# Streaming-encoder layer on one core: PSUM bank sets of the down products swapped, left halves of the final norm moved into the last product

## The chip, the cores and the metric

The kernel runs on one core of a Trainium2 chip. The metric is the time of one execution in microseconds (us), as the device measures it; lower is better. Three executions of the kernel before took 1205.53, 1206.18 and 1206.33 us.

The engines are named as the profile names them: PE is TensorE (matmuls; PEld are its weight loads), DVE is VectorE, ACT is ScalarE, POOL is GpSimd, SP issues the transfers (DMAs). A line such as L1103 is a line of the kernel before unless the text says otherwise.

## The reference, cut to what matters

The layer is a retention and convolution mixer, then a gated MLP, then a last RMS norm. The change touches only the end of the second part and the norm (SEQ = 1024, D_MODEL = 1024, D_FF = 2816):

```python
def rms_norm(x, g):
    xf = x.astype(jnp.float32)
    y = xf * lax.rsqrt(jnp.mean(xf * xf, axis=-1, keepdims=True) + EPS)
    return (y * g.astype(jnp.float32)).astype(x.dtype)
...
        u = causal_dwconv(h @ w_up, conv_ffn_w, conv_ffn_b)
        ua, ub = jnp.split(u, 2, axis=-1)
        x = x + gt2[:, None, :] * ((jax.nn.silu(ua) * ub) @ w_down)
    return rms_norm(x, final_g)
```

## The kernel before, in words

**Precision.** Every fp32 matmul is three matmuls: each operand is split into a rounded high part (`_h`, a cast on ACT, L99 or L1079) and a low part (`_l`, a subtraction on DVE, L100 or L1080), and `mm3` adds high x high, high x low and low x high.

**Up-projection.** `up` makes one 128-row slice of the MLP at a time: `ua` and `ub` (128 x 1024 each) lie in the two PSUM tiles of `m2k`, two banks each. They are read by the convolution (`conv3`: one activation on ACT, L816, then two multiply-adds on DVE, L85; into `act` from `ua`, into `tb` from `ub`), then by silu and a multiplication (L1001). That is done 22 times; slices are taken in pairs (j, j + 11).

**Down-projection by seven products.** The product of the activations (1024 x 2816) with `w_down` (2816 x 1024) is taken as a 2 x 2 block product with seven block products instead of eight (Strassen's scheme in Winograd's form), numbered 1 to 7. The sums and differences of the quarters are made on DVE in `acts_side` (tiles `sc`) and `weights_side` (tiles `tc`; the weights `wd` are first multiplied by `gt2` on POOL, L1029). All operands are written to DRAM (`keep`, L971). One operand `op_p_j` is a 128 x 1024 tile: left half the activations' side, right half the weights' side.

**A product.** `product(p, ps, start)` runs over j = 0..10. `operands` loads `op_p_j` from DRAM (L1076, a ring of eight buffers; the first three into other tiles), casts it on ACT (L1079) and subtracts on DVE (L1080); there are four buffers for the high parts and four for the low. `step_mm` then does three 128 x 512 matmuls for each of the four row blocks i = 0..3, so 12 per operand and 132 per product. The result of a product is four PSUM banks, one per row block.

**Bank sets.** PSUM has two sets for these: `banks_m` takes the two `m2k` tiles (two row blocks share a tile of two banks), `banks_r` takes four `r1k` tiles of one bank each. The products run in the order 1, 6, 2, 7, 5, 4, 3. Products 1 and 2 accumulate in the set `pa`, 6 in `pb`, 7 and 4 in `pc`, 5 and 3 in `pd`. Before the change `pa` and `pd` come from `banks_m`, `pb` and `pc` from `banks_r`. Waits are set by tile: a matmul into a tile waits for every earlier reader of that tile. Between products ACT copies `pa` to `p1` (L1110), DVE and POOL add results into `x1` (`add_to`, L1103 and L1116).

**The end.** `x1` is the residual stream, eight row blocks `tb` of 128 x 1024. Row blocks 4 to 7 are complete before product 3, row blocks 0 to 3 get their right halves from it. Its last four operands (j = 7..10) are all split first; then for each row block i the 12 matmuls of j = 7..10 are done, so that the blocks finish one after the other. `final(tb)` normalises a row block: square and sum on ACT (L162, a 128 x 1024 activation), two small POOL operations (L156 scale and add, L157 power) that give `r`, one multiplication on DVE by `r` and `fg` (the norm's gain; L1138), and one store (L1139). For row block 3 `final_last` does it in halves (L1141 to L1157): left half squared and multiplied by `fg` early, the right half after its addition, then left half scaled on DVE (L1154), right half on ACT (L1155).

**What sets the order.** The matmuls keep program order; so does everything that is wrapped in `pin`. The rest is ordered by a scheduler when the program is built, each engine's instructions and SP's transfers as one queue in order.

## Time and profile before

| | |
|---|---|
| runs, median (lowest to highest) | 1206.18 us (1205.53 to 1206.33) |
| the profiled execution, its own time | 1208.52 us |
| its span, first to last instruction | 1206.7 us |
| mean granted clock of TensorE | 0.990 |
| busy, share of the span: PE / PEld | 1170.5 us, 97% / 969.9 us, 80% |
| busy: DVE / ACT / POOL | 685.0 us, 57% / 392.0 us, 32% / 208.2 us, 17% |
| bytes moved by DMA | 183.60 MB, mean 152 GB/s |

How to read it: the span and the profiled execution's own time belong to one execution, and differ by what lies around the span; the runs are others. TensorE is busy nearly all the time, but its matmuls overlap and their ends are modelled, so the share does not say that it runs at its pace: the distance between the starts of matmuls does. A granted clock of 1.00 is 2.4 GHz, 0.50 is 1.2 GHz. An idle time is only worth something where TensorE, or the end of the kernel, waits for it.

### The profile page before, as it was taken

To read this page: it belongs to the slowest core of one execution; us is meant where nothing else is said; L and a number is where in the kernel's file an instruction comes from. 1 tells how busy PE (TensorE), PEld (TensorE's weight loads), DVE (VectorE), ACT (ScalarE), POOL (GpSimd) and SP (SyncE) were. 2 spreads that over 40 slices of the span, in tenths; PEclk is the share of its full clock that TensorE was granted. 3 is DMA by queue.
4 is the path that set the end of the run, shared out by engine and by line. 5 is a ranking of instruction groups with operands and counts; after the bars stand their busy time and mean duration, and the time that the engine had idled before them with its cause. 6 is when DMAs were issued, how large, how long until landed. Compare 5 with 4: busy or idle time off the path is not lost. (4 is left out here: it accounts for less than half of the span.)

```text
span 1206.7 us, 13864 instructions
## 1 busy us (share of the span) xinstructions
PE 1170.5 (97%) x5356; PEld 969.9 (80%) x5356; DVE 685.0 (57%) x891; ACT 392.0 (32%) x508; POOL 208.2 (17%) x181
## 2 busy tenths in 40 slices
PE   5999999999999999999999999999999989999996
PEld 5788888888888887788888888888888878888884
DVE  5856577555532677646535555454553664555564
ACT  5760123231221345622222222212222224333352
POOL 3503243100000134410110110110111010430021
PEclk9999999999999999999999999999999989999999
DMA  9932422235411254345525534545453358555552
GB/s 271 291 105 70 140 86 78 84 103 165 144 40 56 92 206 155 106 140 175 184 96 175 192 114 157 183 132 182 157 175 122 140 222 300 192 192 193 193 190 87
DMA packets 135677, 183.60 MB, mean 152 GB/s; under 512 B 6948, under 2 KB 85180, under 8 KB 135612
## 3 DMA queue, kind: packets, MB, share of 16 engines
q1 hardware_dynamic: 135612, 182.72, 45.7%
q8 instruction: 42, 0.69, 0.2%
q14 instruction: 23, 0.19, 0.0%
HBM read 138.13 MB, written 44.56 MB: 151 GB/s over the span
## 5 line engine op out<-in xcount | busy, mean ns | idle before, releaser
L113 PE MATMUL ub<-h,wb_h 128*128 128x512 f32 x704 | 217.7, 390 | 0.0
L113 PE MATMUL ua<-h,wa_h 128*128 128x512 f32 x704 | 217.1, 389 | 0.4 <-DVE h L920 0.3
L113 PEld LDWEIGHTS ua<-h,wa_h 128*128 128x128 f32 x704 | 132.2, 188 | 28.5 <-issue 0.6
L113 PEld LDWEIGHTS ub<-h,wb_h 128*128 128x128 f32 x704 | 132.6, 189 | 27.4
L1080 DVE TENSOR_TENSOR op_l<-ring,op_h 128x1024 fp32r<-128x1024 f32 x74 | 94.3, 1275 | 87.1 <-ACT op_h L1079 87.1
L113 PE MATMUL ub<-h,wb_l 128*128 128x512 f32 x352 | 137.2, 390 | 0.0
L113 PE MATMUL ua<-h,wa_l 128*128 128x512 f32 x352 | 136.9, 389 | 0.0
L1029 POOL TENSOR_TENSOR wd<-wd,gt 128x1024 f32<-128x1024 f32 x22 | 54.4, 2492 | 424.8 <-DMA wd<-in_w_down_dram 424.8
L1079 ACT CAST op_h<-ring 128x1024 fp32r<-128x1024 f32 x74 | 78.1, 1055 | 124.9 <-PE pa L113 38.8
L100 DVE TENSOR_TENSOR wb_l<-wb,wb_h 128x1024 fp32r<-128x1024 f32 x22 | 33.6, 1528 | 136.6 <-ACT wb_h L99 136.6
L113 PE MATMUL po<-wo_h,mix 128*128 128x512 f32 x256 | 82.0, 395 | 0.0
L99 ACT CAST wa_h<-wa 128x1024 fp32r<-128x1024 f32 x22 | 23.2, 1054 | 168.5 <-PE ua L113 168.5
L113 PEld LDWEIGHTS ub<-h,wb_l 128*128 128x128 f32 x352 | 66.2, 188 | 13.8
L113 PEld LDWEIGHTS ua<-h,wa_l 128*128 128x128 f32 x352 | 66.1, 188 | 13.6
L100 DVE TENSOR_TENSOR wa_l<-wa,wa_h 128x1024 fp32r<-128x1024 f32 x22 | 28.4, 1291 | 61.2 <-ACT wa_h L99 61.2
L85 DVE SCALAR_TENSOR_TENSOR tb<-ub,fcol,tb 128x1023 f32<-128x1023 f32 (+1 forms) x44 | 56.2, 1278 | 3.0 <-ACT tb L816 2.3
L85 DVE SCALAR_TENSOR_TENSOR act<-ua,fcol,act 128x1023 f32<-128x1023 f32 (+1 forms) x44 | 56.3, 1279 | 0.8
L113 PEld LDWEIGHTS po<-wo_h,mix 128*128 128x128 f32 x256 | 48.1, 188 | 10.4 <-DVE y L836 0.4
L99 ACT CAST wb_h<-wb 128x1024 fp32r<-128x1024 f32 x22 | 23.2, 1054 | 92.5 <-PE ub L113 92.5
L113 PE MATMUL po<-wo_l,mix 128*128 128x512 f32 x128 | 49.9, 390 | 0.0
L99 ACT CAST wo_h<-wo 128x1024 fp32r<-128x1024 f32 x24 | 25.1, 1049 | 62.5 <-PE pgb L113 16.1
L998 ACT ACTIVATE act<-act 128x1024 f32<-128x1024 f32 x22 | 23.3, 1061 | 61.3 <-DVE act L85 61.3
(266 smaller groups left out, 2370.0 us busy)
## 6 DMA issues: line engine op xcount, KB each, us to landing
ring<-op SPq DMA_DIRECT2D x74, 512.0 KB
wo<-in_w_out_dram SPq DMA_DIRECT2D x24, 512.0 KB
wa<-in_w_up_dram SPq DMA_DIRECT2D x22, 512.0 KB
wb<-in_w_up_dram SPq DMA_DIRECT2D x22, 512.0 KB
op<-sc SPq DMA_DIRECT2D x44, 256.0 KB
wd<-in_w_down_dram SPq DMA_DIRECT2D x22, 512.0 KB
op<-tc SPq DMA_DIRECT2D x44, 256.0 KB
op<-act SPq DMA_DIRECT2D x33, 256.0 KB
```

Of the source, the lines that this page charges most:

```text
L85: return nc.vector.scalar_tensor_tensor(out=o, in0=i0, scalar=s, in1=i1, op0=ALU.mult, op1=ALU.add)
L99: c = nc.scalar.copy(hi, src)
L100: d = nc.vector.tensor_tensor(out=lo, in0=src, in1=hi.bitcast(F32), op=ALU.subtract)
L113: pin(nc.tensor.matmul(ps, st, mv, start=start, stop=stop, skip_group_check=more))
L998: nc.scalar.activation(ta, ta, AF.Silu)
L1029: nc.gpsimd.tensor_tensor(out=t, in0=t, in1=gt2, op=ALU.mult)
L1079: nc.scalar.copy(hi, raw)
L1080: nc.vector.tensor_tensor(out=lo, in0=raw, in1=hi.bitcast(F32), op=ALU.subtract)
```

## The change

It does two things.

1. The bank sets change places: `pa` (products 1 and 2) and `pd` (5 and 3) now come from `banks_r`, one tile per row block; `pb` (6) and `pc` (7 and 4) from `banks_m`.
2. `final_last` is gone, and row blocks 0 to 3 are all normalised in halves. While the last product runs, the left half of each is squared on ACT, its sum scaled on POOL and its values multiplied by `fg` on DVE. After a block's last matmul `out_sum` adds the right half, squares it, makes `r` on POOL and multiplies the right half by `fg`. `out_scale`, called one block later (after the next block's `out_sum`), scales the left half on DVE and the right half on ACT, and stores each half by itself. Nearly all of these are pinned in this order.

```diff
-    pa = banks_m("pa")
+    def square_half(tb, c, junk, name):
+        ss = cst.tile([P, 1], F32, tag="ss", name=name, bufs=6)
+        pin(nc.scalar.activation(junk, x1[:, tb, half[c]], AF.Square, accum_out=ss))
+        return ss
+
+    pa = banks_r("pa")
     product(1, pa, True)
...
-    pb = banks_r("pb")
+    pb = banks_m("pb")
     product(6, pb, True)
...
-    pb = banks_r("pc")
+    pb = banks_m("pc")
     product(7, pb, True)
...
-    pa = banks_m("pd")
+    pa = banks_r("pd")
     product(5, pa, True)
...
-    def final_last(tb, ps):
...
     tail = {j: operands(3, j) for j in range(KB, NK)}
     for tb in range(4, 8):
         final(tb)
+
+    ys, s0 = {}, {}
+    for tb in range(4):
+        ys[tb] = w4(f"y_out_{tb}")
+        s0[tb] = square_half(tb, 0, ys[tb][:, half[0]], f"ss3_{tb}_0")
+        pin(nc.gpsimd.tensor_scalar(out=s0[tb], in0=s0[tb], scalar1=1.0 / D, scalar2=EPS, op0=ALU.mult, op1=ALU.add))
+        l = x1[:, tb, half[0]]
+        pin(nc.vector.tensor_tensor(out=l, in0=l, in1=fg[:, half[0]], op=ALU.mult))
+
+    rs = {}
+
+    def out_sum(tb):
+        pin(add_to(tb, 1, pa[tb]))
+        s1 = square_half(tb, 1, ys[tb][:, half[1]], f"ss3_{tb}_1")
+        r = cst.tile([P, 1], F32, tag="rstd1", name=f"r3_{tb}", bufs=6)
+        pin(nc.gpsimd.tensor_scalar(out=r, in0=s1, scalar1=1.0 / D, scalar2=s0[tb], op0=ALU.mult, op1=ALU.add))
+        pin(nc.gpsimd.tensor_tensor(out=r, in0=r, in1=nhalf[:, 0:1], op=ALU.pow))
+        rs[tb] = r
+        g = x1[:, tb, half[1]]
+        pin(nc.vector.tensor_tensor(out=g, in0=g, in1=fg[:, half[1]], op=ALU.mult))
+
+    def out_scale(tb):
+        y = ys[tb]
+        pin(nc.vector.tensor_scalar(out=y[:, half[0]], in0=x1[:, tb, half[0]], scalar1=rs[tb], scalar2=None, op0=ALU.mult))
+        pin(nc.scalar.activation(y[:, half[1]], x1[:, tb, half[1]], AF.Copy, scale=rs[tb]))
+        for c in half:
+            nc.sync.dma_start(out[tb * P : (tb + 1) * P, c], y[:, c])
+
     for i in range(4):
         for j in range(KB, NK):
             step_mm(pa, tail[j], j, i, False)
-        if i < 3:
-            add_to(i, 1, pa[i])
-            final(i)
-        else:
-            final_last(i, pa[i])
+        out_sum(i)
+        if i:
+            out_scale(i - 1)
+    out_scale(3)
```

The instructions that move stand in three places.

On PE at the start of product 1, the last matmul of the up-projection and the first row blocks of operand 0. Before, with `pa_6909` and `pa_6910` the two tiles of the m set:

```order
L113 MATMUL ub_6819<-h_1_3543,wb_l 128x512
L113 MATMUL pa_6909<-op_0_h 128x512 [waits DVE_49,Activation_49]
L113 MATMUL pa_6909<-op_0_l,op_0_h 128x512
L113 MATMUL pa_6909<-op_0_h,op_0_l 128x512
L113 MATMUL pa_6909<-op_0_h 128x512
L113 MATMUL pa_6909<-op_0_l,op_0_h 128x512
L113 MATMUL pa_6909<-op_0_h,op_0_l 128x512
L113 MATMUL pa_6910<-op_0_h 128x512 [waits DVE_49,Activation_49]
```

Now, with `pa_6909` to `pa_6912` the four tiles of the r set:

```order
L113 MATMUL ub_6819<-h_1_3543,wb_l 128x512
L113 MATMUL pa_6909<-op_0_h 128x512
L113 MATMUL pa_6909<-op_0_l,op_0_h 128x512
L113 MATMUL pa_6909<-op_0_h,op_0_l 128x512
L113 MATMUL pa_6910<-op_0_h 128x512
L113 MATMUL pa_6910<-op_0_l,op_0_h 128x512
L113 MATMUL pa_6910<-op_0_h,op_0_l 128x512
L113 MATMUL pa_6911<-op_0_h 128x512
```

No matmul of operand 0 waits for DVE or ACT any more; the matmuls and their order are the same. In the same way the waits on DVE of the first matmul of row blocks 1 and 3 in product 3's tail are gone.

On DVE at the end of the up-projection, after the two multiply-adds of the last `tb` (L85): `op_3_l` to `op_6_l` are the low parts of product 1's operands, `act` is the last activation, `sc` and `tc` are the sums of its two sides.

```order
 L85 SCALAR_TENSOR_TENSOR tb_6869<-ub_6819,fcol,tb_6869 128x1022
+L1080 TENSOR_TENSOR op_4_l<-ring,op_4_h 128x1024
 L1001 TENSOR_TENSOR act_6868<-act_6868,tb_6869 128x1024
-L1005 TENSOR_TENSOR tc_6896<-wd_10_6890 128x512
+L1005 TENSOR_TENSOR tc_6896<-wd_10_6893,wd_10_6890 128x512
 L1005 TENSOR_TENSOR sc_6878<-act_6868,sc_6878 128x512
 L1005 TENSOR_TENSOR sc_6878<-act_6748,act_6868 128x512
 L1005 TENSOR_TENSOR sc_6878<-act_6868,sc_6878 128x512
-L1005 TENSOR_TENSOR tc_6896<-wd_10_6893,wd_10_6890 128x512
-L1080 TENSOR_TENSOR op_4_l<-ring,op_4_h 128x1024
 L1005 TENSOR_TENSOR tc_6896<-tc_6896,wd_10_6890 128x512
+L1005 TENSOR_TENSOR tc_6896<-wd_10_6890 128x512
+L1005 TENSOR_TENSOR tc_6896<-wd_10_6893,tc_6896 128x512
 L1080 TENSOR_TENSOR op_5_l<-ring,op_5_h 128x1024
-L1005 TENSOR_TENSOR tc_6896<-wd_10_6893,tc_6896 128x512
 L1080 TENSOR_TENSOR op_6_l<-ring,op_6_h 128x1024
```

`op_4_l` moved up by six instructions, the last `tc` moved ahead of `op_5_l`.

On DVE at the very end. Before (L1103 additions, L1138 scaling of a whole row block):

```order
L1103 TENSOR_TENSOR x_2997<-pd_7702,x_2997 128x512 [waits PE_49]
L1138 SCALAR_TENSOR_TENSOR y_out_8291<-x_2997,r_1_8294,fg 128x1024 [waits Activation_49,Pool_49]
L1103 TENSOR_TENSOR x_2997<-pd_7703,x_2997 128x512 [waits PE_49]
L1138 SCALAR_TENSOR_TENSOR y_out_8312<-x_2997,r_2_8315,fg 128x1024 [waits DMAHW7_49,Activation_49,Pool_49]
L1147 TENSOR_TENSOR x_2997<-x_2997,fg 128x512 [waits Activation_49]
L1103 TENSOR_TENSOR x_2997<-pd_7703,x_2997 128x512 [waits PE_49]
L1150 TENSOR_TENSOR x_2997<-x_2997,fg 128x512 [waits Activation_49]
L1154 TENSOR_SCALAR y_out_last<-x_2997,r_last 128x512 [waits DMAHW0_49,Pool_49]
```

Now (lines of the changed kernel; L1173 is the product with `fg`, L1177 the scaling of a left half):

```order
L1103 TENSOR_TENSOR x_2997<-pd_7702,x_2997 128x512 [waits PE_49]
L1173 TENSOR_TENSOR x_2997<-x_2997,fg 128x512 [waits Activation_49]
L1177 TENSOR_SCALAR y_out_8262<-x_2997,r_1_8311 128x512 [waits Pool_49]
L1103 TENSOR_TENSOR x_2997<-pd_7703,x_2997 128x512 [waits PE_49]
L1173 TENSOR_TENSOR x_2997<-x_2997,fg 128x512 [waits Activation_49]
L1177 TENSOR_SCALAR y_out_8267<-x_2997,r_2_8334 128x512 [waits DMAHW7_49,Pool_49]
L1177 TENSOR_SCALAR y_out_8272<-x_2997,r_3_8357 128x512 [waits DMAHW0_49,Pool_49]
```

The scaling of a block now stands behind the next block's addition, not ahead of it, and is half as wide.

## Rows read from the trace of the kernel before

**Rows 1.** Waits of PE: engine, line, waited for: us in total, times, longest us

```profile
PE pa L113 <- DVE tb L85: 3.4, 1, 3.4
PE pd L113 <- DVE x L1103: 3.2, 2, 2.4
```

**Rows 2.** Timeline of PE, product 1: start us, us, line, operation [idle before <-releaser]

```profile
978.14 0.39 PE L113 MATMUL pa<-op_h 128*128 128x512 f32 x1
...
979.27 0.39 PE L113 MATMUL pa<-op_h,op_l 128*128 128x512 f32 x1
983.08 0.76 PE L113 MATMUL pa<-op_h 128*128 128x512 f32 x1 [3.42 <-DVE tb L85]
...
1014.65 0.39 PE L113 MATMUL pb<-op_h 128*128 128x512 f32 x1
```

**Rows 3.** Windows at product 1: stretch, us, busy of PE, PEld, DVE, ACT, POOL, PEclk, DMA

```profile
980.00:983.00 3.00, 0.00 (x0) 0.00 (x0) 2.93 (x4) 0.27 (x1) 0.95 (x1) 0.90 1.02 415
983.00:984.00 1.00, 0.92 (x2) 0.83 (x3) 1.00 (x1) 0.00 (x0) 1.00 (x1) 0.50 0.45 176
...
990.00:995.00 5.00, 5.00 (x24) 4.11 (x23) 5.00 (x7) 2.11 (x2) 0.00 (x0) 1.00 1.04 383
```

**Rows 4.** Timeline of DVE after the last up-projection

```profile
980.34 2.59 DVE L85 SCALAR_TENSOR_TENSOR tb<-ub,fcol,tb 128x1023 f32<-128x1023 f32 x2
982.97 2.53 DVE L1001 TENSOR_TENSOR act<-act,tb 128x1024 f32<-128x1024 f32 x1
985.42 2.88 DVE L1005 TENSOR_TENSOR tc<-wd 128x512 f32<-128x512 f32 x1
...
991.77 0.68 DVE L1005 TENSOR_TENSOR tc<-tc,wd 128x512 f32<-128x512 f32 x1
992.37 1.21 DVE L1080 TENSOR_TENSOR op_l<-ring,op_h 128x1024 fp32r<-128x1024 f32 x1
```

**Rows 5.** Timeline of POOL in the same stretch

```profile
982.05 5.70 POOL L1029 TENSOR_TENSOR wd<-wd,gt 128x1024 f32<-128x1024 f32 x2 [46.14 <-DMA wd<-in_w_down_dram]
```

**Rows 6.** Timeline of PE, product 3: its first matmul, and its tail

```profile
1164.26 0.39 PE L113 MATMUL pd<-op_h 128*128 128x512 f32 x1
...
1183.30 0.39 PE L113 MATMUL pd<-op_h 128*128 128x512 f32 x1
...
1187.38 0.50 PE L113 MATMUL pd<-op_h 128*128 128x512 f32 x1 [0.78 <-DVE x L1103]
...
1192.72 0.39 PE L113 MATMUL pd<-op_h,op_l 128*128 128x512 f32 x1
1195.53 0.50 PE L113 MATMUL pd<-op_h 128*128 128x512 f32 x1 [2.42 <-DVE x L1103]
...
1198.19 0.39 PE L113 MATMUL pd<-op_h,op_l 128*128 128x512 f32 x1
```

**Rows 7.** Timeline of DVE in product 3 and at the end

```profile
1174.54 1.28 DVE L1138 SCALAR_TENSOR_TENSOR y_out<-x,r,fg 128x1024 f32<-128x1024 f32 x1 [0.44 <-POOL r L157]
...
1197.65 1.29 DVE L1138 SCALAR_TENSOR_TENSOR y_out<-x,r,fg 128x1024 f32<-128x1024 f32 x1 [2.18 <-POOL r L157]
...
1199.46 0.68 DVE L1103 TENSOR_TENSOR x<-pd,x 128x512 f32<-128x512 f32 x1
...
1202.42 0.49 DVE L1154 TENSOR_SCALAR y_out_last<-x,r_last 128x512 f32<-128x512 f32 x1 [0.80 <-POOL r_last L1153]
```

**Rows 8.** Windows in product 3 and at the end, columns as in rows 3

```profile
1150.00:1180.00 30.00, 30.00 (x134) 24.85 (x133) 20.56 (x20) 15.79 (x19) 8.15 (x8) 1.00 0.51 181
...
1193.00:1195.50 2.50, 0.11 (x1) 0.00 (x0) 1.89 (x2) 0.00 (x0) 0.55 (x1) 1.00 0.00 0
...
1199.00:1203.00 4.00, 0.00 (x0) 0.00 (x0) 2.32 (x4) 1.30 (x3) 1.24 (x2) 0.73 0.33 131
```

**Rows 9.** Timelines of SP and ACT: loads of product 1's operands from `op_8` on, and its cast

```profile
994.58 25.65 SPq L1076 DMA_DIRECT2D ring<-op  x16
...
998.73 1.05 ACT L1079 CAST op_h<-ring 128x1024 fp32r<-128x1024 f32 x1 [1.86 <-DMA ring<-op]
```

More of the change, by code (lines that the diff above doesn't have):

```diff
@@ L1139, in final @@
         nc.sync.dma_start(out[tb * P : (tb + 1) * P, :], y)
-    def final_last(tb, ps):
-        y = w4("y_out_last")
-        xs = x1[:, tb]
-        ss = [cst.tile([P, 1], F32, name=f"ss3_last_{i}") for i in range(2)]
-        nc.scalar.activation(y[:, half[0]], xs[:, half[0]], AF.Square, accum_out=ss[0])
-        nc.gpsimd.tensor_scalar(out=ss[0], in0=ss[0], scalar1=1.0 / D, scalar2=EPS, op0=ALU.mult, op1=ALU.add)
-        nc.vector.tensor_tensor(out=xs[:, half[0]], in0=xs[:, half[0]], in1=fg[:, half[0]], op=ALU.mult)
-        add_to(tb, 1, ps)
-        nc.scalar.activation(y[:, half[1]], xs[:, half[1]], AF.Square, accum_out=ss[1])
-        nc.vector.tensor_tensor(out=xs[:, half[1]], in0=xs[:, half[1]], in1=fg[:, half[1]], op=ALU.mult)
-        r = cst.tile([P, 1], F32, name="r3_last")
-        nc.gpsimd.tensor_scalar(out=r, in0=ss[1], scalar1=1.0 / D, scalar2=ss[0], op0=ALU.mult, op1=ALU.add)
-        nc.gpsimd.tensor_tensor(out=r, in0=r, in1=nhalf[:, 0:1], op=ALU.pow)
-        nc.vector.tensor_scalar(out=y[:, half[0]], in0=xs[:, half[0]], scalar1=r, scalar2=None, op0=ALU.mult)
-        nc.scalar.activation(y[:, half[1]], xs[:, half[1]], AF.Copy, scale=r)
-        for c in half:
-            nc.sync.dma_start(out[tb * P : (tb + 1) * P, c], y[:, c])
     KB = NK - 4
```

## The prediction

> **What bounds the kernel now.** I read the waits of TensorE first, since it is busy for 97% of the span: what it waits for is nearly all that can be won. Two waits of that list lie where the change works: 3.4 us in product 1 on VectorE's `tb` (the convolution that reads the last `ub`), and 3.2 us in two pieces, the longer 2.4, on the additions of line 1103 [rows 1].
>
> Then the timeline of TensorE at product 1. The reader is to see that the six matmuls of blocks 0 and 1 go, the last at 979.27, that the third block starts only at 983.08, and that the next product starts at 1014.65 [rows 2]. At full pace 84 matmuls of product 3 take 1164.26 to 1183.30, 0.2267 us each, so an operand (12) takes 2.72 and a product (132) 29.92 [rows 6]. Product 1 took 1014.65 - 978.14 = 36.51, so it lost 6.59. Only 3.81 - 0.23 = 3.58 of that is the gap; the windows show the rest: the granted clock is 0.90 over 980 to 983, 0.50 (1.2 GHz) in 983 to 984, and 1.00 (2.4 GHz) again from 990 [rows 3]. So about 3.0 us are the half clock after the pause.
>
> Last the tail, where product 3 finishes block after block. Block 1 starts at 1187.38 after a wait, and from 1192.72 to 1195.53, block 2 to block 3, it is 2.81 instead of 0.23 [rows 6]. From 1183.30 to 1198.19 stand 47 steps, 10.65 at full pace and 14.89 in fact: 4.24 lost, of which about 0.4 is the late `op_10` in block 0. After the last matmul (1198.19 + 0.39) the addition that needs it starts only at 1199.46, since VectorE scales block 2 from 1197.65 on [rows 7].
>
> **The change, part by part.** *The swap at product 1.* `pa` now lies in the r banks, free since before the up-projection, and the two waits at its start are gone. The 6.59 go, unless operands are late next. An operand is needed every 2.72 us from 978.14 and its low part one matmul later. The first three were split early, `op_3` before 980.34 [rows 4]. `op_4`, now ahead of the last multiplication of the activations, is needed at 989.2 and takes the place of the row 982.97 to 985.42 [rows 4]: in time. `op_5` is what I expect late. Between the end of `tb` at 982.97 and `op_5` VectorE does the same work as before in another order, plus one subtraction of `tc` that stood behind `op_5`: 992.37 - 991.77 = 0.60 more. Before, `op_5` started at 992.37 [rows 4]; now at 992.97, done with 1.21 at 994.2. TensorE wants it at 978.14 + 5 x 2.72 + 0.23 = 991.97 and resumes at about 994.3: a stall of 2.3. Bounds: none, if VectorE is less held up than before (it lost some 3.5 us there: 2.53 and 2.88 where such work takes 1.2 and 0.68 [rows 4], beside GpSimd's two multiplications [rows 5]), and 3.6, if it is held until these end at 987.75 and has 1.2 + 1.2 + 7 x 0.60 + 1.21 = 7.8 left, to 995.5. I take 2.3, because the rows show this very work.
> The Trainium skill bears on that wait ("SBUF — State Buffer", Who interferes with whom): a VectorE instruction with two SBUF inputs and a GpSimd one that reads SBUF exclude each other for a whole instruction. The rows agree in size, 2.88 - 0.68 = 2.2 beside 5.70 for two. By that rule at its hardest the stall is 3.6, and the sum below 1.3 us worse.
>
> After it `op_6` and the rest need 1.2 each in 2.72: VectorE catches up. The swap at the other products costs nothing: each set was read a whole product earlier. Reading m-bank blocks in pairs delays an addition by one block, 0.7 us, with a product's 29.92 to spare.
>
> *The tail.* One tile per bank takes away both waits on line 1103: 4.24 - 0.4 = 3.8 us. The last addition no longer queues behind a 1.29 us scaling: 1199.46 - 1198.58 = 0.88, less 0.05 for the signal, 0.8 more. In the new order VectorE's work for a block (addition, product with `fg`, the half scaling of the block before) is some 1.7 us in a block's 2.72, so it is idle when block 3 ends. The chain behind the last addition (square, two operations on GpSimd, scaling, transfer) is the old one.
> Against it: the half scaling of block 2 (0.49, as the row at 1202.42 [rows 7]) now stands before the last scaling and may hold GpSimd's power, 0 to 0.49, I take 0.2; and block 2's output leaves about 1 us before block 3's, not 4: 0 to 1 us, I take 0.2, as the two halves start apart. Sum of the tail: 3.8 + 0.8 - 0.4 = 4.2.
>
> *The four early half squares and products.* ScalarE gets four squares of 512 columns, each under the 1.05 of a 1024-column cast [rows 9], VectorE four products of 0.60, both between 1170 and 1182. In 1150 to 1180 they are busy 15.79 and 20.56 of 30 us [rows 8], so the idle time is cover: 14.2 and 9.4. The tightest is `op_8`: before, the scaling with `r_7` ended at 1174.54 + 1.28 = 1175.8 [rows 7]; I allow 1.5 more for its later square, then `op_6`, a product, `op_7`, three products and `op_8` (3 x 1.2 + 4 x 0.60 = 6.0) end at 1183.3, and it is wanted at 1183.30 + 3 x 0.2267 + 0.23 = 1184.2. If that cover is gone, block 0 stalls by that much, at most 2.4. GpSimd's four added `ss` operations stand behind the last `r_7`, and nothing waits for them before block 0's square. The two later `y_out` buffers wait for the stores of `y_out_4` and `y_out_5`; ScalarE stops there with `op_7` behind it, needed some 8 us later. The queue of transfers has eight half stores for four others at the end: eight issues of about 0.4 us in some 11 us.
>
> **The sum.** 6.6 - 2.3 + 4.2 = 8.5 us. The profiled execution took 1208.52 (span 1206.7, 1.8 around it), so such a one would show 1200.0. The runs' median lies 2.3 below it, at 1206.18; the same difference gives **1197.7**. About 0.2%, 2.4 us, is what a measurement of this kernel tells from no change.
>
> **The rivals.** *The clock falls in the new stall.* For it: after the 3.58 pause it was at half for some 6 us, costing 3.0. Against it: the 2.58 pause of the tail (2.81 - 0.23) left it at 1.00 [rows 8]. But the idle stretch after the last matmul has 0.73 over 1199 to 1203 [rows 8], so it fell there between 2 and 3 us after the work ended. A stall of 2.3 lies at the edge. Price 1.5 to 3.0, taken as 3.0: 1200.7. The skill ("TensorE: Matmul & The Clock Gate", HAM oscillation) says that waits between bursts of matmuls put the array back to the low clock and each burst starts cold; by that rule 1200.7 is the time. The pause of product 1 agrees, the pause of the tail doesn't.
>
> *No stall.* If VectorE isn't held up, `op_5` comes in time: 8.5 + 2.3 = 10.8, 1195.4. The rows of that work speak against it.
>
> *Only one of the gains.* VectorE is held to the bound of 3.6 and the clock falls by 3.0: the pause only moves and the tail's 4.2 are left, 1202.0. (That is the lock of the skill's SBUF page with its clock rule.) Or the tail waits on something new and the start's 4.3 are left: 1201.9.
>
> *Slower.* One transfer decides it: product 1 reads `op_9` from DRAM, and that load is issued behind the last store of `tc`, about 993.6. Its low part is ready at 993.6 + L + 1.05 + 1.23 and wanted at 978.14 + 9 x 2.72 + 2.3 + 0.23 = 1005.2: late if its landing L is over 9.3. The nearest row, `op_8` issued at 994.58 and cast at 998.73 [rows 9], gives L = 4.15. With L = 18 the stall is 8.7, and 3.0 for the clock: 11.7 - 8.5 = 3.2 slower, 1209.4. From L of 17 it is over the bound. Only a transfer four times as slow would do it.
>
> That the change doesn't do what it says is excluded for the waits: the instruction order has none where they were.
>
> **How the numbers follow.** Forecast 0.45; clock falls 0.30; no stall 0.08; one gain alone 0.13; slower 0.04. The first three lie within 1195.4 and 1200.7; with the bounds of the tail (0.4 below, 1.3 above) the range is 1195.0 to 1202.0, which leaves out the slower case and some of the one before it. Faster by over 0.2% is all but the last case and a rest for several bounds together: 0.93; within 0.2% 0.03; slower 0.04.
>
> **What would show it.** Right: the waits of TensorE have no `pa` on `tb` and no `pd` on line 1103; the third block of product 1 starts at 978.6; a wait of about 2.3 on `op_l` before `op_5`, then steady 2.72 steps; product 1 takes about 32.2; the tail's 47 steps take about 11, and the last addition starts within 0.1 of the last matmul. The clock around 994 to 1000 tells forecast from first rival. Wrong: `op_l` waits at other operands, in the tail above all, a wait on `ring`, or ScalarE waiting for a store at `y_out`.

## The result and the profile after

| | before | after |
|---|---|---|
| runs beside each other, median (lowest to highest) | 1206.11 us (1205.53 to 1206.33, 4 runs) | 1196.99 us (1196.71 to 1199.93, 4 runs) |
| ratio | | 0.9934, 95% interval 0.9922 to 0.9947 |
| the profiled execution: own time, span | 1208.52, 1206.7 us | 1197.04, 1195.2 us |

The change makes the kernel faster by 0.5 to 0.8%, well over the 0.2% that can be told; the forecast was 1197.7 us, with a range of 1195.0 to 1202.0. Of every kernel one execution was profiled, so a row below tells of that execution.

The head of the page after. TensorE's work is what it was, 5356 matmuls, in 11.5 us less; VectorE has 6 instructions more than its 891 before, ScalarE 9 more than its 508.

```profile
span 1195.2 us, 13885 instructions
...
PE 1166.3 (98%) x5356; PEld 967.5 (81%) x5356; DVE 687.8 (58%) x897; ACT 394.1 (33%) x517; POOL 212.8 (18%) x184
```

The only wait of TensorE in the changed kernel, from the start of product 1 to the end, as the waits list it (columns as in [rows 1]). Both waits of [rows 1] are gone; this one is new.

```profile
PE pa L113 <- DVE op_l L1080: 1.9, 1, 1.9
```

TensorE in product 1 after (columns as in [rows 2]). The third block starts 1.36 us after the first, at full pace, where it had waited 3.42. The new wait stands before the second matmul of `op_5`, which wants its low part: 990.65 - 988.32 = 2.33 where a step is 0.23. Product 1 takes 1006.88 - 974.72 = 32.16 instead of 36.51.

```profile
974.72 0.39 PE L113 MATMUL pa<-op_h 128*128 128x512 f32 x1
...
976.08 0.39 PE L113 MATMUL pa<-op_h 128*128 128x512 f32 x1
...
988.32 0.39 PE L113 MATMUL pa<-op_h 128*128 128x512 f32 x1
990.65 0.50 PE L113 MATMUL pa<-op_l,op_h 128*128 128x512 f32 x1 [1.95 <-DVE op_l L1080]
...
1006.88 0.39 PE L113 MATMUL pb<-op_h 128*128 128x512 f32 x1
```

The windows around this wait (columns as in [rows 3]): the granted clock stays at 1.00 (2.4 GHz) through the wait and behind it, where [rows 3] had 0.50.

```profile
985.00:990.00 5.00, 3.70 (x17) 2.73 (x15) 5.00 (x9) 2.10 (x2) 0.00 (x0) 1.00 0.80 297
990.00:992.00 2.00, 1.35 (x6) 1.13 (x7) 2.00 (x3) 0.00 (x0) 0.00 (x0) 1.00 1.03 382
992.00:994.00 2.00, 2.00 (x11) 1.65 (x10) 2.00 (x2) 0.00 (x0) 0.00 (x0) 1.00 1.06 340
994.00:996.00 2.00, 2.00 (x11) 1.65 (x10) 0.00 (x1) 0.00 (x0) 0.00 (x0) 1.00 1.08 264
```

VectorE in front of the wait, then GpSimd beside it. The reader is to see that VectorE has no idle time from the last `tb` to the end of `op_5` (the first of the four `op_l` in the last row), and that two instructions there are long: the subtraction of `op_4` with 2.47 and the last multiplication of the activations with 3.42. The same two kinds take 1.23 (at 964.89) and 1.22 (at 957.78) elsewhere. Beside them GpSimd works on the last pair's weights.

```profile
976.92 2.60 DVE L85 SCALAR_TENSOR_TENSOR tb<-ub,fcol,tb 128x1023 f32<-128x1023 f32 x2
979.43 2.47 DVE L1080 TENSOR_TENSOR op_l<-ring,op_h 128x1024 fp32r<-128x1024 f32 x1
981.82 3.42 DVE L1001 TENSOR_TENSOR act<-act,tb 128x1024 f32<-128x1024 f32 x1
985.17 0.68 DVE L1005 TENSOR_TENSOR tc<-wd,wd 128x512 f32<-128x512 f32 x1
...
988.78 0.68 DVE L1005 TENSOR_TENSOR tc<-wd,tc 128x512 f32<-128x512 f32 x1
989.38 4.62 DVE L1080 TENSOR_TENSOR op_l<-ring,op_h 128x1024 fp32r<-128x1024 f32 x4
```

```profile
978.41 5.75 POOL L1029 TENSOR_TENSOR wd<-wd,gt 128x1024 f32<-128x1024 f32 x2 [45.89 <-DMA wd<-in_w_down_dram]
```

TensorE in product 3 after, against [rows 6]: first matmul; then blocks 0, 1, 2 and 3 of the tail; last matmul. The tail's 47 steps take 11.09 where they took 14.89; 0.41 of the 0.44 that is still lost lies in block 0, whose 12 steps take 1178.65 - 1175.52 = 3.13 instead of 2.72, since `op_10` is late there.

```profile
1156.47 0.39 PE L113 MATMUL pd<-op_h 128*128 128x512 f32 x1
...
1175.52 0.39 PE L113 MATMUL pd<-op_h 128*128 128x512 f32 x1
...
1178.65 0.40 PE L113 MATMUL pd<-op_h 128*128 128x512 f32 x1
...
1181.39 0.39 PE L113 MATMUL pd<-op_h 128*128 128x512 f32 x1
...
1184.12 0.39 PE L113 MATMUL pd<-op_h 128*128 128x512 f32 x1
...
1186.61 0.39 PE L113 MATMUL pd<-op_h,op_l 128*128 128x512 f32 x1
```

VectorE behind the last matmul (L1173 is the product with `fg`, L1177 the scaling of a left half, first of block 2 and then of block 3). The addition starts 0.42 after the start of the last matmul, 0.03 after its end at 1187.00; the last scaling starts 3.02 after the addition, as in [rows 7] (2.96), and the span ends 5.15 after that, where it was 4.28.

```profile
1187.03 0.69 DVE L1103 TENSOR_TENSOR x<-pd,x 128x512 f32<-128x512 f32 x1
1188.51 0.69 DVE L1173 TENSOR_TENSOR x<-x,fg 128x512 f32<-128x512 f32 x1 [0.79 <-ACT y_out L1107]
1189.12 0.49 DVE L1177 TENSOR_SCALAR y_out<-x,r 128x512 f32<-128x512 f32 x1
1190.05 0.49 DVE L1177 TENSOR_SCALAR y_out<-x,r 128x512 f32<-128x512 f32 x1 [0.43 <-POOL r L1170]
```

So the end of the kernel falls into six stretches that can be compared over all kernels of this study, each from the same kind of row: the start of product 1; product 1 (to the first matmul of product 6); the products between (to the first matmul of product 3); product 3 (first to last start of a matmul); from there to the start of the last addition; to the start of the last scaling; to the end of the span.

| kernel | product 1 starts | product 1 | between | product 3 | to the addition | to the scaling | to the end | product 1 to the end |
|---|---|---|---|---|---|---|---|---|
| before | 978.14 | 36.51 | 149.61 | 33.93 | 1.27 | 2.96 | 4.28 | 228.56 |
| after | 974.72 | 32.16 | 149.59 | 30.14 | 0.42 | 3.02 | 5.15 | 220.48 |
| e1, swap alone | 974.21 | 34.26 | 149.60 | 30.13 | 1.00 | 5.46 | 4.04 | 224.49 |
| e2, tail alone | 976.04 | 35.23 | 149.60 | 32.28 | 0.43 | 3.01 | 4.41 | 224.96 |
| e3, `op_5` early | 977.14 | 32.20 | 149.60 | 30.13 | 0.42 | 3.02 | 5.19 | 220.56 |
| e4, left halves stored early | 977.34 | 32.51 | 149.60 | 30.13 | 0.43 | 2.97 | 5.22 | 220.86 |
| e5, weights early | 975.01 | 29.92 | 149.60 | 30.13 | 0.42 | 3.02 | 4.60 | 217.69 |
| e6, whole stores | 975.92 | 32.40 | 149.60 | 30.12 | 0.43 | 3.01 | 5.32 | 220.88 |
| e7, e5 and a longer ScalarE | 975.84 | 29.91 | 149.61 | 30.12 | 0.43 | 3.01 | 4.58 | 217.66 |
| e8, e5 and a longer VectorE | 972.84 | 29.92 | 149.60 | 30.14 | 0.42 | 3.02 | 4.26 | 217.36 |
| e9, after and a longer VectorE | 975.09 | 32.34 | 149.60 | 30.13 | 0.43 | 3.02 | 4.29 | 219.81 |
| e10, the kernel of e8 again | 973.22 | 29.92 | 149.60 | 30.16 | 0.43 | 3.02 | 4.25 | 217.38 |

The views give the span to a tenth, so the last two columns are good to 0.05.

The part that was changed gained 228.56 - 220.48 = 8.08 us. The two profiled executions differ by 11.5; the other 3.4 lie ahead of product 1, where the programs do the same work. That start moves from execution to execution: it lies between 974.21 and 978.14 in seven kernels (before, after, e1 to e4, e6) whose up-projection was left alone. Most of it comes early: after 1000 matmuls TensorE is at 212.6 us before and at 209.4 after, so 3.2 of the 3.4 are lost by then, and over all twelve kernels that point lies between 208.1 and 212.6. A part comes near 500 us, where the granted clock drops to 0.50 (1.2 GHz) in nine kernels and stays at 1.00 (2.4 GHz) in e1, e5 and e8: from that point to product 1 these three take 763.8 to 764.3, the others 765.1 to 765.8. A median of four to seven executions carries some of all that, so the experiments are read from the stretches, and from the medians only where these differ by more.

### The profile page after: what moved, and what is told of

The parts are those of the page before. It is cut to its first block, busy times and chain, and to the rows that moved or that the text cites. A ratio compares the mean times of both kernels' runs of the same rounds, so it can differ in the third digit from the quotient of the medians.

```text
span 1195.2 us, 13885 instructions
## 1 busy us (share of the span) xinstructions
PE 1166.3 (98%) x5356; PEld 967.5 (81%) x5356; DVE 687.8 (58%) x897; ACT 394.1 (33%) x517; POOL 212.8 (18%) x184
## 4 chain that ended last, share of the span: by engine, by line
PE 89%; DVE 4%; issue 2%; POOL 2%; ACT 2%; DMA 1%; SPq 1%; POOLq 0%; DVEq 0%
PE ub L113 20%; PE ua L113 20%; PE po L113 5%; PE pc L113 5%; PE pd L113 5%; PE pa L113 4%; PE pg L113 4%; PE pq L113 4%; PE pk L113 4%; PE pgc L113 4%; PE phc L113 4%; PE pgb L113 4%; PE pb L113 3%; PE pv L113 2%; POOL x L904 1%
## 5 line engine op out<-in xcount | busy, mean ns | idle before, releaser
L85 DVE SCALAR_TENSOR_TENSOR tb<-ub,fcol,tb 128x1023 f32<-128x1023 f32 (+1 forms) x44 | 56.2, 1278 | 3.0 <-ACT tb L816 2.3
L85 DVE SCALAR_TENSOR_TENSOR act<-ua,fcol,act 128x1023 f32<-128x1023 f32 (+1 forms) x44 | 56.3, 1280 | 0.8
```

Source lines behind the costliest of these rows:

```text
L85: return nc.vector.scalar_tensor_tensor(out=o, in0=i0, scalar=s, in1=i1, op0=ALU.mult, op1=ALU.add)
```

## The experiments

**e1: the swap alone.** The kernel before, with its old tail and the bank sets exchanged.

```diff
-    pa = banks_m("pa")
+    pa = banks_r("pa")
...
-    pb = banks_r("pb")
+    pb = banks_m("pb")
...
-    pb = banks_r("pc")
+    pb = banks_m("pc")
...
-    pa = banks_m("pd")
+    pa = banks_r("pd")
```

> The bank sets swapped, the old tail (whole row blocks scaled at once, halves for block 3 alone). Theory: the swap alone takes away both places where TensorE waited, the start of product 1 (4.3 us won) and the two waits on line 1103 in the tail (3.8), since one tile per bank is all that these need. TensorE's list of waits then has no pa on tb and no pd on x, and the last matmul comes as early as with the whole change; what is lost is behind the last matmul: the scaling of block 2 (1.28 us, after its own square and power) stands ahead of block 3's last steps, some 2.4 us later than with the new tail. Expected about 1199, 7 us faster than before. Rival: the waits in the tail need the late scaling of the new tail code too; then the two waits (3.2 us) stay and the time is 1201 to 1202.

Measured: 1200.66 us (1200.49 to 1201.63, 5 runs), ratio 0.9958 (0.9946 to 0.9970). Product 3 takes 30.13, with no wait on L1103: the swap by itself takes both waits out of the tail, and the rival, that they need the new code too, falls. Without the new code the last scaling comes 6.46 after the start of the last matmul, where the changed kernel has 0.42 + 3.02 = 3.44, so 3.02 later (2.4 were expected): VectorE and ScalarE work through block 2's norm and both halves of block 3 first. The last two additions are one row of e1, and the last one, the second of the two, starts at 1189.20:

```profile
1188.60 1.28 DVE L1103 TENSOR_TENSOR x<-pd,x 128x512 f32<-128x512 f32 x2
```

And product 1 takes 34.26, 2.10 more than after, with a wait that is 0.48 longer; that is why the time lies above the 1199 that were expected. TensorE's row and the windows of e1 show it:

```profile
990.63 0.50 PE L113 MATMUL pa<-op_l,op_h 128*128 128x512 f32 x1 [2.43 <-DVE op_l L1080]
```

```profile
990.00:991.00 1.00, 0.37 (x2) 0.33 (x3) 1.00 (x2) 0.00 (x0) 0.00 (x0) 1.00 1.04 381
991.00:992.00 1.00, 1.00 (x6) 0.82 (x5) 1.00 (x2) 0.00 (x0) 0.00 (x0) 0.98 1.02 381
992.00:994.00 2.00, 2.00 (x7) 1.52 (x6) 1.98 (x2) 0.00 (x0) 0.00 (x0) 0.50 1.08 332
994.00:996.00 2.00, 2.00 (x7) 1.59 (x6) 0.00 (x0) 0.00 (x0) 0.00 (x0) 0.66 0.90 266
```

After a wait of 2.43 the granted clock fell to 0.50 (1.2 GHz), some 1.3 us after the matmuls had resumed. That is the prediction's first rival, met in this kernel.

**e2: the tail alone.** The changed kernel with the four bank sets put back.

```diff
-    pa = banks_r("pa")
+    pa = banks_m("pa")
...
-    pa = banks_r("pd")
+    pa = banks_m("pd")
```

> The new tail on the old bank sets. Theory: product 1 loses its 6.6 us as before (pause on tb, then half clock), and in the tail TensorE still waits twice on line 1103, because two row blocks share a tile, but only for an addition that starts at once, some 0.8 us of idle time each instead of 0.8 and 2.4: TensorE's tail is 1.6 to 1.9 us shorter than before, and the last addition no longer queues (0.8). Less about 0.9 for the two stores that collide at the end: 1.5 to 2.5 us faster than before, about 1204. Rival: the tail code is what makes the tail short, whatever the banks: then 3.7 us faster than before, 1202.4, and no wait over 0.5 us on line 1103.

Measured: 1202.77 us (1200.74 to 1204.01, 7 runs), ratio 0.9971 (0.9960 to 0.9982). The waits of TensorE in e2:

```profile
PE pa L113 <- DVE tb L85: 3.4, 1, 3.4
...
PE pd L113 <- DVE x L1103: 1.6, 2, 0.8
```

The pause of product 1 is back as it was, 3.42 long. The clock behind it is not: the granted clock is at 0.50 from 982.4 to 989.2 before and only from 981.2 to 984.6 in e2. A window of e2 and one of the kernel before, some 5 and 4 us after the matmuls have resumed (at 980.98 and 983.08):

```profile
986.00:990.00 4.00, 4.00 (x20) 3.28 (x19) 4.00 (x6) 1.35 (x2) 0.34 (x1) 1.00 0.50 187
```

```profile
987.00:990.00 3.00, 3.00 (x10) 2.32 (x9) 3.00 (x4) 0.06 (x1) 0.75 (x1) 0.63 0.33 122
```

So product 1 takes 35.23 instead of 36.51, and e2 is 3.6 us faster than before, by its time where the rival put it (3.7). Its waits are those of the theory: from product 3's start to the end it gains 2.31, within the 1.5 to 2.5 expected, and the other 1.28 is the clock. In the tail the two waits are now 0.8 each instead of 0.8 and 2.4: with the scaling behind the next addition the longer one shrinks, and only the swap takes away the rest. Both parts of the change work on the same waits of L1103, so their gains there don't add: e1 gains 3.80 in product 3, e2 1.65, both together 3.79.

**e3: `op_5` ahead of the last sums.** The last pair's sums are emitted behind product 1's first six operands.

```diff
...
-        acts_side(j, acts[j], acts[j + NK])
-        weights_side(j)
+        if j < NK - 1:
+            acts_side(j, acts[j], acts[j + NK])
+            weights_side(j)
...
-    product(1, pa, True)
+    product(1, pa, True, range(6))
+    acts_side(NK - 1, acts[NK - 1], acts[2 * NK - 1])
+    weights_side(NK - 1)
+    product(1, pa, True, range(6, NK))
```

> The changed kernel with the first six operands of product 1 written ahead of the last pair's sums, so that on VectorE the low part of operand 5 stands directly behind the last multiplication of the activations and ahead of the sums sc and tc. Theory: the 1.95 us wait of product 1 (2.1 with what follows it) is the order of VectorE alone; it goes, and nothing takes its place, as the low part of operand 6 ends about when it is wanted (991.2 against 991.3 in the changed kernel's time). Expected 1194.7 to 1195.2, product 1 in 29.9 to 30.3 us. Rival: the work in front of operand 6 is the same as it was in front of operand 5, so the wait only moves to operand 6 or 7 and the time stays at 1197; second rival: the later sums delay the stores and the loads of operands 9 and 10, and TensorE waits there on ring.

Measured: 1195.91 us (1195.05 to 1199.44, 5 runs), ratio 0.9917 (0.9903 to 0.9931). The wait before `op_5` is gone, but product 1 takes 32.20 as before it: two shorter waits of 0.70 and 0.77 stand before `op_6` and `op_9`. The median is 1.1 below that of the changed kernel and its lowest run too, yet from product 1 to the end it takes 220.56 against 220.48, so this is no gain. The theory, 29.9 to 30.3 for product 1, falls; the rival, that the wait moves on, is what happened. VectorE in e3 tells where the time goes:

```profile
981.85 3.41 DVE L1081 TENSOR_TENSOR op_l<-ring,op_h 128x1024 fp32r<-128x1024 f32 x1
985.18 3.42 DVE L1001 TENSOR_TENSOR act<-act,tb 128x1024 f32<-128x1024 f32 x1
988.53 1.21 DVE L1081 TENSOR_TENSOR op_l<-ring,op_h 128x1024 fp32r<-128x1024 f32 x1
```

It is not the place of `op_5` in the order: the subtraction of `op_4` and the last multiplication are long again. Moving work behind them only moves the wait.

**e5: the last pair's weights early.** What makes them long? GpSimd's two multiplications, or something else in that stretch (the transfers, the casts)? e5 calls the weights' side of the last pair before its up-projection.

```diff
     for j in range(NK):
+        if j == NK - 1:
+            weights_side(j)
         for i in range(2):
...
-        weights_side(j)
+        if j < NK - 1:
+            weights_side(j)
```

> The changed kernel with one thing moved: the weights' side of the last pair (its two loads, GpSimd's two multiplications, the four sums tc and their stores) is emitted before the last two up-projection slices instead of behind them. Theory (VectorE is slow at op_4 and at the last multiplication of the activations because GpSimd's two multiplications run beside them, and the tc sums lie between them and op_5): the two VectorE instructions that took 2.47 and 3.42 us go back to about 1.2 each, op_5's low part is ready well before TensorE wants it, the wait of 1.95 us before op_5 is gone, product 1 takes 29.9 to 30.3 us instead of 32.16, and from the start of product 1 to the end it is 218.2 to 218.6 us instead of 220.48; the time is about 1195. Rival 1 (those two instructions are slow for another reason, the transfers or ScalarE's cast beside them): they still take over 2 us each; then only the four sums leave the path and the wait shrinks without the durations doing so. Rival 2 (the lock only moves): an instruction of the convolution beside GpSimd's multiplications takes 2 to 4 us instead of 1.2 and TensorE waits for it in the up-projection, so that what product 1 gains is lost before it.

Measured: 1193.48 us (1192.78 to 1194.46, 4 runs), ratio 0.9895 (0.9877 to 0.9913). VectorE behind the last `tb`, then GpSimd, whose two multiplications for this pair (the last of the three, and the one alone) now end 23 us ahead of product 1 instead of 9 behind its start:

```profile
979.72 1.22 DVE L1083 TENSOR_TENSOR op_l<-ring,op_h 128x1024 fp32r<-128x1024 f32 x1
980.86 1.22 DVE L1001 TENSOR_TENSOR act<-act,tb 128x1024 f32<-128x1024 f32 x1
981.99 1.22 DVE L1083 TENSOR_TENSOR op_l<-ring,op_h 128x1024 fp32r<-128x1024 f32 x1
```

```profile
928.41 8.10 POOL L1029 TENSOR_TENSOR wd<-wd,gt 128x1024 f32<-128x1024 f32 x3 [38.75 <-DMA wd<-in_w_down_dram]
949.55 2.39 POOL L1029 TENSOR_TENSOR wd<-wd,gt 128x1024 f32<-128x1024 f32 x1 [13.04 <-DMA wd<-in_w_down_dram]
```

The two instructions take 1.22 each, `op_5` is split from 981.99 on, done at 983.2 where TensorE wants it at 988.8, and product 1 takes 29.92, its full pace. Rival 1 falls, since the two are short with a cast of ScalarE still beside them (at 980.65) and the DMA engines busier than in the changed kernel (0.58 of the stretch 979.72 to 983.20, against 0.49 of 979.43 to 985.24). So does rival 2: the list of TensorE's waits is empty from 880 to the end. The first of the two multiplications does meet a busy VectorE (933.12 to 936.51 in the trace, 3.39 instead of 2.39), but no instruction of the convolution beside it takes more than 1.28. From product 1 to the end e5 takes 217.69, 0.5 below what was expected: the last stretch is shorter too, 4.60 instead of 5.15, which was not forecast.

**e4: left halves stored early.** The other term to look into is the 0.87 at the end. First guess: block 2's store collides with block 3's. e4 scales and stores each block's left half by itself, right behind the next block's addition, and the right half later.

```diff
...
-            out_scale(i - 1)
-    out_scale(3)
+            out_right(i - 1)
+    out_left(3)
+    out_right(3)
```

> The changed kernel with the scaling of a left half placed directly behind the next block's addition on VectorE (ahead of its product with fg), its store issued there. Block 2's left half is then stored about 1.4 us earlier. Theory: the end of the changed kernel, 5.15 us from the last scaling to the end against 4.28 before, is longer because block 2's two stores still move when block 3's are issued; with one of them out of the way the stretch falls to 4.3 to 4.8 and the time by 0.4 to 0.9, to 1196.1 to 1196.6. Rival: two half stores at the end take as long as that by themselves (their last one is issued late or lands slowly): the stretch stays at 5.1 and the time at 1197. TensorE's part of the tail is untouched by it.

Measured: 1200.25 us (1196.67 to 1201.24, 6 runs), ratio 0.9946 (0.9932 to 0.9961); from product 1 to the end 220.86. The last stretch takes 5.22, though block 2's left half now leaves ahead of the rest. That speaks against the collision as the cause. The median lies 3.3 above that of the changed kernel, which neither guess had; in the profiled execution (1199.95) 2.62 of it are the later start of product 1.

**e6: whole stores.** The profile's DMA part for the last 6 us has something else. After, with the share of the DMA engines and the rate in 40 slices of 0.15 us:

```profile
DMA  0000089998999969999999991000000000000000
GB/s 0 0 0 0 0 328 410 382 423 328 396 396 396 314 219 355 355 369 410 355 355 423 369 342 28 14 14 27 14 27 0 0 0 0 0 0 0 0 0 0
...
q1 hardware_dynamic: 576, 1.05, 47.5%
q14 instruction: 1, 0.01, 0.3%
```

The stores run at full rate up to the 24th slice, then bytes trickle in at 14 to 28 GB/s for six slices, 0.9 us. And there is one packet of what the profile calls an instruction queue (q14), 2.9 us before the end, which the last 6 us of the kernel before do not have. Which engine's program is it? e6 stores blocks 0 to 2 whole, which takes three transfers out of SP's program.

```diff
-        for c in half:
+        for c in half if tb == 3 else (slice(0, 1024),):
             nc.sync.dma_start(out[tb * P : (tb + 1) * P, c], y[:, c])
```

> The changed kernel with row blocks 0 to 2 stored whole (one transfer of 512 KB each, three instructions fewer on SP); block 3 still in halves. In the changed kernel the last scaling starts 5.15 us before the end, in the kernel before 4.28, and its profile has a packet of the instruction queue 2.85 us before the end, which the kernel before has not; behind it the bytes of the stores trickle in at 14 to 27 GB/s for 0.8 us. Theory (the packet, a piece of some engine's program, holds one DMA engine up, and it is there because a program has grown): if SP's program is the one that grew over an edge, the packet is gone and the last scaling starts 4.3 us before the end, 0.8 less, about 1196.1; if ScalarE's or another's is, the packet and the 5.15 stay, within 0.2. Rival (block 2's store collides with block 3's): now block 2's store starts later, when both its halves are scaled, so that more of it lies beside block 3's; the last scaling starts 5.2 to 5.6 us before the end and no trickle of one engine is seen.

Measured: 1198.51 us (1194.55 to 1199.39, 6 runs), ratio 0.9931 (0.9914 to 0.9948). The packet stays, 2.7 us before the end, the trickle too, and the stretch takes 5.32. SP has as many instructions as in the kernel before (783 in the trace), so it is not SP's program. The 5.32 lies where the rival, the collision, had it too (5.2 to 5.6); the trickle speaks against that, and e9 decides.

**e7 and e8: which program.** In e5 the stretch was 4.60 and no packet lay in it, with the same tail. e7 and e8 are e5 with eight small copies that nothing uses, on ScalarE or on VectorE.

```diff
+    dummy = cst.tile([P, 8], F32, name="dummy")
...
+            for n in range(8):
+                nc.scalar.copy(dummy[:, n : n + 1], nhalf[:, 0:1])
```

(In e8 the last line is `nc.vector.tensor_copy` with the same operands. In both the scheduler put the copies near the start.)

> e5 (last pair's weights early) with eight copies of one element per partition added to ScalarE's program, which nothing uses. In e5 the packet of the instruction queue at the end is gone and the last scaling starts 4.60 us before the end, though it has the same tail and as many instructions that compute; only waits that are instructions of their own are fewer: the trace has 802 instructions of ScalarE against 807 in the changed kernel, 1217 of VectorE against 1218, and 794 and 1217 in the kernel before. Theory (ScalarE's program is the one that grew over the edge, between 802 and 807): with 810 the packet is back in the last 6 us, a trickle of one engine follows the stores, and the last scaling starts 5.1 to 5.3 us before the end; product 1 stays at 29.9. Rival (it is VectorE's program, between 1217 and 1218, or chance): no packet at the end, 4.5 to 4.7 us.

> e5 with the same eight copies added to VectorE's program instead. Theory (ScalarE's program): no packet of the instruction queue in the last 6 us, the last scaling starts 4.5 to 4.7 us before the end. Rival (VectorE's program is the one that grew over the edge): the packet is back and the last scaling starts 5.1 to 5.3 us before the end. If neither this run nor the one with ScalarE's copies shows the packet, it does not hang on the length of a program and its cause stays open.

Measured: e7 1195.30 us, e8 1192.01 us (one run each). The theory of ScalarE falls: with 810 instructions no packet came back, and the stretch stayed at 4.58. VectorE's copies did move a packet, but not as the rival had it: it now lies at 1171.4, 19 us before the end, and the stretch takes 4.26. With all kernels set side by side, the last packet follows the count of VectorE's instructions (all in the trace, with those that only wait or signal, which the head of a page leaves out):

| VectorE's instructions in the trace | kernels | last packet of the instruction queue, against the end of the span |
|---|---|---|
| 1214 | e1 | 1.3 us behind it |
| 1217 | before, e5, e7 | 0.6, 0.6 and 0.3 us behind it |
| 1218 | after, e3, e4, e6 | 2.9, 3.0, 2.8 and 2.7 us ahead of it |
| 1221 | e2 | 4.8 us ahead |
| 1225 | e8, e10 | 18.8 and 18.9 us ahead |
| 1226 | e9 | 18.9 us ahead |

**e9: the changed kernel with a longer VectorE program.** The same eight copies, in the changed kernel itself.

```diff
+    dummy = cst.tile([P, 8], F32, name="dummy")
+    for n in range(8):
+        nc.vector.tensor_copy(dummy[:, n : n + 1], nhalf[:, 0:1])
```

> The changed kernel itself with eight copies of one element per partition, used by nothing, added to VectorE's program near its start. So far the last packet of the instruction queue stood, in seven kernels, where VectorE's count of instructions says: with 1214 1.2 us behind the end, with 1217 0.1 to 0.6 behind it, with 1218 2.7 to 3.1 us before it, with 1221 4.9 before it, with 1225 19 us before it; ScalarE's count does not order them. Theory (the packet is a piece of VectorE's program, asked for when VectorE comes to a certain instruction, and costs time only where it meets the last stores): with 1226 it lies about 20 us before the end, and the last scaling starts 4.2 to 4.6 us before the end instead of 5.15; product 1 stays near 32.2 to 32.5 with its wait for op_5; from the start of product 1 to the end about 219.7 to 220.2 us. Rival (the 0.87 comes of the half stores colliding, and e5 lost it only by its other timing): the packet moves but the last scaling still starts 5.1 to 5.3 us before the end.

Measured: 1197.06 us (1193.82 to 1198.98, 4 runs), ratio 0.9922 (0.9901 to 0.9942). The last 6 us of e9:

```profile
GB/s 410 301 14 0 0 0 0 0 0 0 96 382 355 369 423 383 382 369 382 301 232 369 396 382 396 355 396 382 396 232 14 0 0 0 0 0 0 0 0 0
...
q1 hardware_dynamic: 645, 1.16, 51.8%
```

No packet, no trickle: the stores run at full rate to their end, and the last scaling starts 4.29 before the end of the span, as in the kernel before, with the same eight half stores in the same order. Eight instructions more make the stretch 0.86 shorter, and the rival, that the half stores collide, falls. The packets of the trace say where the 0.86 lies: the last bytes of the stores end 2.9 us after the start of the last scaling in before, e1, e5 and e7 to e10, 3.0 in e2, 3.6 to 3.7 in after, e3 and e4, and 4.1 in e6. The q14 packet itself is busy for 0.3% of 16 engines' 6 us, which is 0.3 us of one engine; why the stores come 0.8 later is not shown. Since all runs of e9 spread over 5 us, its median shows nothing of that; the stretch does.

**e10: both.** The kernel of e8, timed.

> The last pair's weights early and the eight copies on VectorE together, the kernel of e8 again, now timed against the kernel before. Theory: product 1 29.9 and the last scaling 4.2 to 4.6 us before the end, 217.3 to 217.7 from the start of product 1, so 3 us less than the changed kernel's 220.48: a median near 1193.5, within one of that of e5. Rival (the copies delay VectorE's early work and TensorE with it): product 1 starts over 978 and the median is above 1195.

Measured: 1194.52 us (1192.16 to 1197.05, 6 runs), ratio 0.9905 (0.9887 to 0.9924). From product 1 to the end 217.38, as expected, and product 1 starts at 973.22, so the copies delay nothing. The median is 1.04 above that of e5, a little more than expected; in time the two can't be told apart, in the stretches e10 is 0.3 shorter. Both are faster than the changed kernel by about 3 us in the part that differs. The 0.3 lies behind the stores, whose last bytes come 2.9 after the last scaling in both. There, among the instructions that close the program, VectorE's last DRAIN starts 0.45 us after the semaphore instruction before it in e5 and 0.09 in e8. It takes 136 ns in e5 and 19 in e8 (the shorter of the two in each row below), and 139, 136, 19 and 19 in before, e7, e9 and e10:

```profile
L1209 DVEq DRAIN  x2: 136/331/526, 1188.1 to 1192.3; - x2
```

```profile
L1213 DVEq DRAIN  x2: 19/272/526, 1186.0 to 1189.8; - x2
```

## Why the prediction was right

| term | predicted | measured |
|---|---|---|
| product 1: loss before, less the new stall | 6.6 - 2.3 = 4.3 | 36.51 - 32.16 = 4.35 |
| tail: TensorE's waits on L1103 | 3.8 | 33.93 - 30.14 = 3.79 |
| tail: last addition no longer queued | 0.8 | 1.27 - 0.42 = 0.85 |
| half scaling of block 2 in the way | -0.2 (0 to -0.49) | 2.96 - 3.02 = -0.06 |
| block 2's output ahead of block 3's | -0.2 (0 to -1) | 4.28 - 5.15 = -0.87 |
| sum | 8.5 | 8.1 |

The mechanism was right in the two large terms, and the tail's came as computed. In the first some luck is in the size: of the 6.6, about 3.0 was the half clock of the one execution that was profiled, and behind the same wait of 3.42 it cost only about 1.7 in e2 (35.23 - 29.92 - 3.58).

**The stall.** The prediction had 10.0 us of VectorE's work between the end of `tb` and the start of `op_5` (982.97 to 992.97). Measured are 979.43 to 989.38, 9.95. That held although the lock fell on other instructions: before, on the multiplication and the first `tc` (2.53 and 2.88 [rows 4]), now on `op_4` and the multiplication. To take the sum of a stretch from the row that shows it, with its disturbance, was better than to add undisturbed durations (1.2 + 1.2 + 7 x 0.60 = 6.6). It is not exact: in the five kernels that keep this order (after, e1, e4, e6, e9) the idle time before `op_5` is 1.95 to 2.43. The bound of 3.6 needed VectorE to be shut out until GpSimd ended. Instead the two engines took turns: one multiplication of GpSimd takes 2.39 alone (e5), two take 4.78, and the row has 5.75, nearly one VectorE instruction more. The trace has the two apart. The first ends at 980.82, and `op_4` ends at 981.90; the second runs from 980.77 to 984.16, 3.39, and the multiplication of the activations ends at 985.24: both times VectorE needs about 1.1 more, its own time. The Trainium skill ("SBUF — State Buffer", Who interferes with whom) says that the one that comes second waits for a whole instruction: 3.42 less 1.22 is 2.20, near the 2.39 of one multiplication, and e5 shows the 1.22 come back when GpSimd works elsewhere. The trace agrees; the prediction's reading of the rule "at its hardest" left out that GpSimd waits as well.

**The clock.** The first rival did not come true in the profiled execution of the changed kernel, but it was as near as the prediction put it: e1, with the same product 1, met it, so it is in part luck that the forecast came true here and not the rival. In product 1 the clock held after waits of 1.95 (after), 2.11 (e9), 2.19 (e6) and 2.28 (e4), and fell with 2.43 (e1) and 3.42 (before, e2). The wait of 2.42 in the tail of the kernel before [rows 6] did not bring it down [rows 8]. The length of a wait alone does not decide it. Near 498 us TensorE waits before the same transposes, 2.12 in the changed kernel and 2.11 in e5; the clock fell in the first (0.76 over the window) and held in the second:

```profile
497.74 1.09 PE L121 MATMUL x1T<-small,t 128*128 128x128 f32 x8 [2.12 <-DVE t L907]
498.00:505.00 7.00, 7.00 (x33) 5.87 (x32) 3.38 (x8) 3.55 (x7) 2.76 (x2) 0.76 0.00 0
```

```profile
499.52 1.09 PE L121 MATMUL x1T<-small,t 128*128 128x128 f32 x8 [2.11 <-DVE t L907]
498.00:505.00 7.00, 5.47 (x32) 4.78 (x33) 3.92 (x9) 4.50 (x9) 2.20 (x5) 1.00 0.00 0
```

Where it fell behind the new wait (e1) it cost 34.26 - 32.16 = 2.1, less 0.48 for the longer wait: about 1.6, at the low end of the rival's 1.5 to 3.0. Of the Trainium skill's page ("TensorE: Matmul & The Clock Gate", HAM oscillation) the trace bears out that pauses between matmuls can lower the clock, not that every burst behind a pause starts cold. The page tells that of a kernel whose waits are longer than this one; the prediction left that condition out, so "by that rule 1200.7 is the time" made the rule harder than it is.

**The cover.** Nothing that was costed at nothing came out of its cover. ScalarE waited 0.81 for a store at the fourth `y_out`, as the prediction had seen it might, and the cast behind it was still in time; `op_10` is late in block 0 by 0.4, as before; `op_9` of product 1 was not late at all in the changed kernel.

**The term that was mis-sized** is the step "block 2's output leaves about 1 us before block 3's, not 4: 0 to 1 us, I take 0.2". It measured 0.87, near its bound, and its mechanism was wrong. The stores themselves cost nothing that shows (4.29 in e9 with the same stores, 4.28 before). What cost 0.87 is a packet of the instruction queue among the last stores: moved away by eight VectorE instructions, it took 0.86 with it (e9). The trace of before could not have told its price, though it has 23 such packets in its span. The next lay 0.6 us behind the end and so cost nothing; in the four kernels with 1218 VectorE instructions instead of 1217 it lies among the stores. No run changed that count by one alone. The other -0.2, for GpSimd, was nearly free.

**The total.** The sum missed the changed part by 0.4 (8.5 against 8.1) and the median by 0.7. These are different things: the medians differ by 9.1, 1.0 more than the stretches of the two profiled executions. With one profile each it is not shown where that 1.0 lies; that the median came out so near is in part luck.

What stays open: why VectorE's last DRAIN is longer in before, e5 and e7; why a packet of 0.3 us delays the stores by 0.8; what moves the first 210 us by up to 4.5 us from one execution to the next; and what, beside the length of a wait, decides whether the clock falls.

## What to carry to other kernels

When a wait goes, count what its releaser's engine still has to do for the next consumer, in the order in which it now stands, and take that time from a row with the disturbance in it: here it gave the new stall within 0.2 us. A wait that names VectorE may really be GpSimd's: moving the consumer forward (e3) only moved the wait, moving GpSimd's work away (e5) removed it. Compare small edits by stretches of the trace and not by medians, if code that was left alone varies by more than the edit is worth.

## What the hardware showed that I had not expected

- While the program runs, packets of an instruction queue are moved: the trace has 23 or 24 of q14 over the span, of 8 KB or so (0.20 MB in 24). When the last one comes follows VectorE's count of instructions: eight copies near the program's start moved it by 16 us towards the start (after to e9), while eight on ScalarE (e7 against e5) moved it by only 0.3.
- One such packet costs 0.86 us when it falls among the last stores (5.15 against 4.29), and nothing that shows 19 us before the end, inside product 3 (30.13 to 30.16 in e8 to e10, 30.14 after). That it holds one DMA engine up, whose share of the stores then comes late, is read from the trickle at 14 to 28 GB/s; no run tried it by itself.
- The clock can fall after the matmuls have resumed: in e1 it was 1.00 in the wait itself and fell 1.3 us behind its end. The same wait can bring it down in one execution and not in another (2.12 and 2.11 near 498 us), and behind the same wait of 3.42 it stayed down for 6.8 us before and 3.4 us in e2.
